# A hybrid decoder layer on one core: a third landing place for x, another step for the value gathers, and the attention's first keys and queries loaded inside the input projection

## The chip, the core and the metric

The kernel runs on one core of a Trainium2 chip. A core has TensorE (PE, matrix products), VectorE (DVE), ScalarE (ACT), GpSimd (POOL) and SyncE (SP, which here only issues transfers); ACT and POOL can issue transfers too. Times are device microseconds (us) of one launch, and the figure compared is the median over runs.

## The reference

One inference step of a one-layer decoder, for a prompt of 2048 new tokens and for 8 samples of 8 new tokens with 8192 cached tokens each. Model width is 1024. Cut to what matters:

```python
z = x @ w_in                                   # one input projection for everything
fq, fk, fv, flogf = ...                        # forgetting attention: 8 heads of 64
mq, mk = silu(conv4(z_qk)); mv, ig, lf, og = ...   # mLSTM: 4 heads of 128
# prompt attention, causal
L = cumsum(flogf)
p = softmax(fq @ fk.T / 8 + L[q] - L[k]);  fox_h = p @ fv
# sample attention over a paged cache (512 pages of 128 tokens) and the 8 new tokens
s_past = q @ k_past.T / 8 + Ln + R;  s_new = ...
p = softmax(concat(s_past, s_new));  o = p @ concat(v_past, v_new)
# mLSTM: chunks of 64 tokens, state C, n, m carried
h = (W * (q @ k.T) @ v + a * q @ C) / den
mix = concat(fox_h, norm(h) * og) @ w_o
x1 = layer_norm(alpha * x + mix)
y  = layer_norm(alpha * x1 + square(relu(x1 @ w1)) @ w2)
```

It returns y for both groups, the new keys, values and log forget values, and the mLSTM and convolution states.

## The kernel before

Precision: every float32 product of the projections is made of three matmuls of split operands (a high and a low part; `split_hi` on ACT, `split_lo` on DVE, both at L154 and L157, the matmuls at L162 to L164). So each weight or x tile is loaded, split on ACT and DVE, and then used by PE.

Stages, in order of time:

- **Input projection**, 0 to about 920 us. The tokens go in four blocks, `BLKS = [[16, 0, 1, 2, 3], [4, 5, 6, 7], [8, 9, 10, 11], [12, 13, 14, 15]]`, where a number is a tile of 128 prompt tokens and 16 stands for the 64 sample tokens. `block_a(bi)` runs, for each block, passes over columns of the weights: mLSTM values (2 passes, with the gates), mLSTM queries and keys (4), output gates (2), attention queries (2) and keys (2), attention values V (2). The passes made token by token go through `natural`, which takes a hook that it calls ahead of each tile; each result is copied from PSUM into a staging tile `st` on ACT and stored. The weights land in `wra` (2 places), loaded by `wload` and split into `whi` and `wlo` (4 places each).
- x lands in the tile `xn`, by `x_load`, issued by SP; `x_turn` splits it into `xh` and `xl`, which the whole block uses. `xn` has 2 landing places, which the gate tiles (`gt`, `rows`) share by their tag.
- Beside the projection's matmuls run two kinds of generators, stepped on by `tick`: `gate_stream`, `m_block` and `m_sample` (mLSTM), and the sample attention (`sample_attention`), which begins in block 0 and runs on in the output projection and the MLP.
- **Prompt attention** `phase_b`, about 920 to 1365 us. It goes over 64 units (8 heads by 8 groups of 256 queries). For each unit: `queries` loads queries (`qn`, two transfers of 64 partitions) and splits them (`qh`, `ql`); `keys` loads 512 keys (`kn`, two transfers) and splits them into `ks`; for the first head it also loads forget values `nl` and values `vn` by pieces of 512 (`forget_values`). `scores` makes `pS` on PE (L945, L946), adds `nl` or the masked diagonal `nd` (made on POOL, L938) and takes row maxima `mx` on DVE; `values` takes the exponential on ACT (S, L973), transposes it on PE (pt, L986) and multiplies with `vn` (po, L995). Scores run one unit ahead of values.
- **Output projection**, about 1365 to 1610 us, and **MLP** to the end.

The sample attention: one `step(n)` after another issues gathers of cached keys (`k_gather`, tile `kT`, L1624) and values (`v_gather`, tile `vt` or `vx`, two gathers each, L1735), both indirect transfers issued by POOL; `qk_step` makes scores (sQ, L1647; sT, L1696), `weights` the transposed probabilities PTs (L1718), and `pv_step` the products with V (sO, L1759). A pair of gathered value tiles has one landing place during the input projection (`vt`) and two afterwards (`vt` and `vx`, once `vx["more"]` is set); `v_room()` says whether one is free. `pv_step` is called at even n from 38 on.

The order on the engines is not the order of the program text: a scheduler lays the instructions out by its own time model, engine by engine, subject to data and to free places, and so carries loads ahead of where they are written. SP runs its queue strictly in order; an entry that waits for its data or for its place holds all that stand behind it. A transfer issued by SP also waits for the eighth transfer before it to have ended, since its completion lanes are used in turn.

At the hand-over from the projection to the prompt attention, block 3's V pass stores 256-wide pieces (`v_prompt`, L574), the last mLSTM chunk makes its output (mn L696, hh on POOL L604, transposed by PE, mm L609, copied by ACT to ot L611, stored to `dmix` L612), and the states C_prompt and n_prompt are stored (L709, L712).

Of the kernel before, what the change touches and what calls it, by code (L numbers as in the profile page):

```python
# [10 lines left out]
F32 = mybir.dt.float32  # L11
# [13 lines left out]
D = 1024  # L25
# [27 lines left out]
def body(ctx, tc, I, O, stages):  # L53
# [152 lines left out]
    for c in W_PASSES:  # L206
        w_at[c] = sum(D * sum(m for _, m in q) for q in w_at)

    es_a = ExitStack()
    pa = es_a.enter_context(tc.tile_pool(name="pa", bufs=1, reuse_waits="tile"))  # L210
# [76 lines left out]
    xns = {}  # L287

    def x_load(*tiles):
        for t in tiles:  # L290
            xns[t] = pa.tile([128, D], F32, name="xn", bufs=2)
            n = 8 * tok_n(t)
            first(SY.dma_start(xns[t][:, :n], I["xs_t"] if t == 16 else I["xp_t"][t]))
# [22 lines left out]
    def gate_stream(bi):  # L316
# [4 lines left out]
        def gates(z, lg, shape, bb):  # L321
            V.tensor_tensor(z, z, bb, op=OP.add)
            gt = pa.tile([128, 1024], F32, name="gt", tag="xn", bufs=2)
            tmp = [gt[:, i * 64:i * 64 + 64].rearrange("p (c g) -> p c g", g=16) for i in range(3)]
# [35 lines left out]
        def rowset(cols, base, n_el, np_, sample):  # L360
            R = [pa.tile([8, 1024], F32, name="rows", tag="xn", bufs=2) for _ in range(2)]
            fr = R[1][:, 0:n_el]
# [73 lines left out]
    def block_a(bi):  # L436
# [18 lines left out]
        def stage(ps, m, n):  # L455
            st = pa.tile([128, 256], F32, name="st", bufs=4)[:m, :n]
            A.copy(st, ps)
            return st

        def turn_next(n):  # L460
            for t in blk[n + 2:n + 3]:
                x_turn(bi, t)
                if bi == 0:
                    x_load(*blk[n + 4:n + 5])

# [105 lines left out]
        for i in range(2):  # L571
            def sink(t, m, ps, i=i):
                d = v_out(t)[:, i * 256:(i + 1) * 256]
                SY.dma_start(d, stage(ps, m, 256))  # L574

            def turn_first(n):
                if n == 0:
                    x_load(*BLKS[bi + 1][0:2])
                if n == len(blk) - 1:
                    x_turn(bi + 1, BLKS[bi + 1][0])  # L580
                    x_load(BLKS[bi + 1][2])
            natural(sink, (1024 + i * 256, 256), hook=None if i == 0 or bi == 3 else turn_first)

# [256 lines left out]
    x_turn(0, 0)  # L840
    x_load(2)
    for bi in range(4):
        g = block_a(bi)
        next(g)
        if bi == 0 and gen:
            acc[0], acc[1] = -12.0, gen
        macc[1].append(m_block(bi))
        mst["open"] = True
        for _ in g:
            pass  # L850
        if bi == 0:
            macc[1].append(m_sample())
        if bi < 3:
            x_turn(bi + 1, BLKS[bi + 1][1])
            x_load(BLKS[bi + 1][3])
    while macc[1]:
# [8 lines left out]
    def phase_b():  # L865
# [47 lines left out]
        def queries(z, g):  # L913

            h = z["h"]
            qn = pb.tile([128, 256], F32, name="qn", bufs=3)
            for d in range(2):
                SY.dma_start(qn[d * 64:d * 64 + 64], dq[h // 2, h % 2 * 64:h % 2 * 64 + 64, g * 256:(g + 1) * 256])
# [108 lines left out]
        Z = {0: dict(h=0)}  # L1027
        kn = keys_load(0, 0)
        queries(Z[0], 0)
# [5 lines left out]
        G.affine_select(dmask, dmask, pattern=[[-1, 128]], compare_op=OP.is_ge, fill=NEG, base=0, channel_multiplier=1)  # L1035
        keys(Z[0], 0, kn)
        sc = {}
        w2_due = [0.0]
        LA = 1
        for n in range(len(units) + LA):  # L1040
# [20 lines left out]
            if n >= LA:  # L1061
                h, g = units[n - LA]
                values(Z[h], g, sc.pop(n - LA))
        es.close()


# [422 lines left out]
def sample_attention(tc, I, O, ps_, pps, cst, ident, dnl, dR, dmix, dqb, vx, kx, pa):  # L1489
# [301 lines left out]
    def step(n):  # L1791
# [3 lines left out]
        g = at(n, 6, 4)  # L1795
# [29 lines left out]
        if g is not None and g < 64:  # L1825
            r_load(g)
        if n >= 35 and (n % 2 == 1 or not vx["live"]):
            while v_room():
                v_gather()
# [73 lines left out]
```

## Time and profile before

| | |
|---|---|
| runs of the kernel | 3286.64, 3292.24, 3301.8 us; median 3292.24 |
| profiled execution | 3288.1 us, span in the profile 3286.4 us |
| PE busy | 3148.6 us (96% of the span), mean granted clock 0.984 |
| DVE, ACT, POOL busy | 2099.1, 1500.7, 912.9 us |
| transfers | 734.37 MB, mean 223 GB/s |
| xn<-xp_t | 16 transfers of 512 KB, SP |
| wra<-w_in | 104 transfers of 512 KB, SP |
| kn<-k_prompt, qn<-dq | 64 of 128 KB, 128 of 64 KB, SP |
| kT gathers, vt gathers (POOL) | 256 and 164, each 1069 ns on POOL |

A line of a group or a timeline reads: start in us (timelines only), time, engine, line, operation, output <- input with its shape, count, and in square brackets the idle time of that engine just before and what ended it. SPq is SP issuing a transfer; its time is that of the issue, with the time for which the queue stood at it, not the transfer's. A row of waits gives the engine and line that waited, what ended the wait, its sum in us, the number of times and the longest.

### The profile page before, as it was taken

The page shows a single profiled execution, that of the slowest core. Times are in us where ns is not written, and L with a number is a line of the kernel's source. Part 1 is how long each engine was busy: PE and PEld are TensorE (multiplying, and loading weights), DVE is VectorE, ACT ScalarE, POOL GpSimd, SP SyncE. Part 2 cuts the span into 40 slices and gives each one's busy share as a digit, 9 for nine tenths or more (in the row PEclk, how much of TensorE's full clock was granted, in tenths as well). Part 3 has the DMA queues.
Part 4 walks back from the last instruction along what each step waited for, and adds up shares of the span by engine and source line. Part 5 has one row for each costly group of instructions (what it writes and reads, how often), then busy time and mean ns, then how long its engine had stood idle before and what let it go on. Part 6 is the DMA issues. An engine that isn't in the chain of part 4 may idle for free.

```text
span 3286.4 us, 58046 instructions
## 1 busy us (share of the span) xinstructions
PE 3148.6 (96%) x21681; PEld 2564.4 (78%) x21681; DVE 2099.1 (64%) x5079; ACT 1500.7 (46%) x2966; POOL 912.9 (28%) x977
## 2 busy tenths in 40 slices
PE   8999998998989999999999999999999999799997
PEld 8998998888856666677677777776777777698895
DVE  6856565355468788644466658656586666856658
ACT  4343343233358888622344345343454444444442
POOL 0121233322324333276433422433333121100000
PEclk9999999999989999999999999999999999999998
DMA  5575766766678675487887878878879666543332
GB/s 186 149 221 177 236 221 216 236 232 198 223 232 226 160 201 136 159 298 253 305 292 273 290 256 298 315 254 327 289 290 343 218 231 211 187 152 119 120 105 100
DMA packets 339698, 734.37 MB, mean 223 GB/s; under 512 B 63640, under 2 KB 177688, under 8 KB 338520
## 3 DMA queue, kind: packets, MB, share of 16 engines
q1 hardware_dynamic: 252856, 416.71, 39.6%
q0 software_dynamic: 83520, 304.12, 26.6%
q10 hardware_dynamic: 3040, 9.83, 0.8%
q8 instruction: 171, 2.80, 0.3%
q14 instruction: 111, 0.91, 0.1%
HBM read 677.71 MB, written 86.38 MB: 233 GB/s over the span
## 4 chain that ended last, share of the span: by engine, by line
PE 45%; DVE 3%; DMA 3%; issue 1%; POOL 1%; ACT 1%; another core or an unknown queue 0%; DVEq 0%; POOLq 0%; ACTq 0%; SPq 0%
PE ph L162 7%; PE ph L163 7%; PE ph L164 7%; PE py L162 6%; PE py L164 5%; PE py L163 5%; PE sO L1759 3%; PE sQ L1647 2%; DMA vt<-cache_v,idxV 1%; DVE wl L157 1%; PE sT L1716 1%; DVE y L1323 1%; DMA kT<-cache_k,idxK 0%; PE pw L163 0%; PE pw L164 0%
## 5 line engine op out<-in xcount | busy, mean ns | idle before, releaser
L157 DVE TENSOR_TENSOR wl<-wr,wh 128x1024 fp32r<-128x1024 f32 x364 | 445.6, 1226 | 376.3 <-ACT wh L154 341.0
L154 ACT ACTIVATE wh<-wr 128x1024 fp32r<-128x1024 f32 x364 | 382.6, 1054 | 321.8 <-PE ph L163 131.1
L162 PE MATMUL ph<-x1h,wh 128*128 128x512 f32 (+1 forms) x1280 | 455.8, 356 | 0.8 <-DVE x1l L157 0.5
L163 PE MATMUL ph<-x1l,wh 128*128 128x512 f32 (+1 forms) x1280 | 453.9, 355 | 0.0
L1624 POOL DMA_INDIRECT kT<-cache_k,idxK x256 | 273.7, 1069 | 640.0 <-PE sQ L1647 578.0
L164 PE MATMUL ph<-x1h,wl 128*128 128x512 f32 (+1 forms) x1280 | 451.3, 354 | 0.0
L162 PE MATMUL py<-wh,hh 128*128 128x512 f32 x896 | 356.8, 400 | 5.9 <-DVE y L1323 2.5
L163 PE MATMUL py<-wl,hh 128*128 128x512 f32 x896 | 351.6, 392 | 0.3 <-issue 0.3
L164 PE MATMUL py<-wh,hl 128*128 128x512 f32 x896 | 349.6, 393 | 1.3 <-DVE hl L157 1.0
L1323 DVE TENSOR_TENSOR y<-y,py 128x512 f32<-128x512 f32 x416 | 280.3, 682 | 69.0 <-PE py L164 55.7
L162 PE MATMUL pm<-xh,whi 128*128 128x256 f32 (+1 forms) x1024 | 301.7, 295 | 1.3 <-issue 0.8
L163 PE MATMUL pm<-xl,whi 128*128 128x256 f32 (+1 forms) x1024 | 297.6, 291 | 2.3 <-issue 2.2
L164 PE MATMUL pm<-xh,wlo 128*128 128x256 f32 (+1 forms) x1024 | 296.8, 290 | 2.8 <-issue 2.8
L162 PEld LDWEIGHTS ph<-x1h,wh 128*128 128x128 f32 x1280 | 241.3, 189 | 40.9 <-issue 7.8
L1735 POOL DMA_INDIRECT vt<-cache_v,idxV x164 | 175.3, 1069 | 340.5 <-PE sO L1759 272.6
L163 PEld LDWEIGHTS ph<-x1l,wh 128*128 128x128 f32 x1280 | 241.5, 189 | 34.2 <-issue 3.7
L164 PEld LDWEIGHTS ph<-x1h,wl 128*128 128x128 f32 x1280 | 241.0, 189 | 34.1 <-issue 3.7
L162 PE MATMUL pm<-whi,xh 128*128 128x256 f32 (+2 forms) x816 | 238.7, 293 | 9.2 <-ACT whi L154 8.3
L163 PE MATMUL pm<-wlo,xh 128*128 128x256 f32 (+2 forms) x816 | 233.9, 287 | 1.6 <-issue 1.0
L164 PE MATMUL pm<-whi,xl 128*128 128x256 f32 (+2 forms) x816 | 233.5, 286 | 0.9 <-issue 0.8
L973 ACT ACTIVATE S<-S,mx 128x512 f32<-128x512 f32 (+2 forms) x320 | 207.8, 653 | 18.2 <-DVE mx L959 15.8
L162 PEld LDWEIGHTS py<-wh,hh 128*128 128x128 f32 x896 | 168.3, 188 | 55.5 <-issue 14.0
(371 smaller groups left out, 6810.5 us busy)
## 6 DMA issues: line engine op xcount, KB each, us to landing
wr<-w SPq DMA_DIRECT2D x224, 512.0 KB
wr<-dw SPq DMA_DIRECT2D x128, 512.0 KB
wra<-w_in SPq DMA_DIRECT2D x104, 512.0 KB
dw<-w POOLq DMA_DIRECT2D x48, 512.0 KB
Rb<-dR SPq DMA_DIRECT2D x128, 128.0 KB
xn<-xp_t SPq DMA_DIRECT2D x16, 512.0 KB
kn<-k_prompt SPq DMA_DIRECT2D x64, 128.0 KB
qn<-dq SPq DMA_DIRECT2D x128, 64.0 KB
```

The lines of the kernel that those rows point to most:

```text
L154: last["ACT"] = A.activation(dst, src, AF.Copy, scale=scale)
L157: r = (eng or V).tensor_tensor(dst, src, hi.bitcast(F32), op=OP.subtract)
L162: T.matmul(ps, wh, xh, start=first, stop=False, skip_group_check=shared)
L163: T.matmul(ps, wh, xl, start=False, stop=False, skip_group_check=shared)
L164: last["PE"] = T.matmul(ps, wl, xh, start=False, stop=stop, skip_group_check=shared)
L973: last["ACT"] = A.activation(sp[:, :w], sp[:, :w], AF.Exp, bias=mx[:, 7:8], accum_out=lp[:, k:k + 1])
L1323: V.tensor_tensor(y, y, ps, op=op)
L1624: G.indirect_dma_start(out=piece(n), out_offset=None, in_=ck, in_offset=IO(ap=idxK[:, b, j // 2, j % 2:j % 2 + 1], axis=0))
L1647: r = T.matmul(pq[h4 * 32:h4 * 32 + 32, hg].rearrange("p (k c) -> p k c", k=2), z["qb"][:, hd], kv, start=(db == 0), stop=(db == 1), skip_ ...
L1716: T.transpose(p[:, f], z["U"][u][:, hg, f].rearrange("p k t -> p (k t)"), ident)
L1735: G.indirect_dma_start(out=vt.rearrange("p f c -> p (f c)"), out_offset=None, in_=cv, in_offset=IO(ap=idxV[:, b, (kt % 4) * 4 + kt // 4, f ...
L1759: after_ = T.matmul(po[r:r + 32], z["PT"][:, hg, 2 * f + g, pg].rearrange("p h q -> p (h q)"), vts[f][:, g, hg * 256:(hg + 1) * 256], star ...
```

## The change

Four edits.

1. `xn`, `gt` and `rows` get 3 places instead of 2 (4 KB of each partition). x loads move: of the next block, two tiles are loaded during the first V pass and one during the second, and the fourth at its end, when the first of them is split; before, two were loaded at the second V pass's first tile, one at its end and one at the block's turn. In block 0 tile 3 is loaded before the block begins, not in its first pass.
2. In `step`, values are gathered at even n instead of odd n when a place is free and another is in use. In the text of `step` the value gathers stand ahead of the key gathers as before.
3. `begin_b` loads the first keys (128x512) and the first queries (128x256) of the prompt attention into tiles of their own (pool `pf`, 3 KB of each partition), from a hook in block 3's last V pass; the attention no longer loads them.
4. The stores of block 3's last V pass are issued by ACT instead of SP.

```diff
+    es_f = ExitStack()
+    pf = es_f.enter_context(tc.tile_pool(name="pf", bufs=1, reuse_waits="tile"))
+    bf = {}
+
+    def begin_b():
+
+        bf["kn"] = pf.tile([128, 512], F32, name="kn0")
+        bf["qn"] = pf.tile([128, 256], F32, name="qn0")
+        for d in range(2):
+            SY.dma_start(bf["kn"][d * 64:d * 64 + 64], O["k_prompt"][0:64, 0:512])
+        for d in range(2):
+            SY.dma_start(bf["qn"][d * 64:d * 64 + 64], dq[0, 0:64, 0:256])
...
-            xns[t] = pa.tile([128, D], F32, name="xn", bufs=2)
+            xns[t] = pa.tile([128, D], F32, name="xn", bufs=3)
...
-            gt = pa.tile([128, 1024], F32, name="gt", tag="xn", bufs=2)
+            gt = pa.tile([128, 1024], F32, name="gt", tag="xn", bufs=3)
...
-            R = [pa.tile([8, 1024], F32, name="rows", tag="xn", bufs=2) for _ in range(2)]
+            R = [pa.tile([8, 1024], F32, name="rows", tag="xn", bufs=3) for _ in range(2)]
...
         def turn_next(n):
             for t in blk[n + 2:n + 3]:
                 x_turn(bi, t)
-                if bi == 0:
-                    x_load(*blk[n + 4:n + 5])
...
                 d = v_out(t)[:, i * 256:(i + 1) * 256]
-                SY.dma_start(d, stage(ps, m, 256))
-
-            def turn_first(n):
-                if n == 0:
-                    x_load(*BLKS[bi + 1][0:2])
-                if n == len(blk) - 1:
+                (A if bi == 3 and i == 1 else SY).dma_start(d, stage(ps, m, 256))
+
+            def turn_first(n, i=i):
+                if n % 2 == len(blk) % 2:
+                    if i == 0 or n < 2:
+                        x_load(BLKS[bi + 1][(i * 2 + n // 2) if n < 4 else 1])
+                if i == 1 and n == len(blk) - 1:
                     x_turn(bi + 1, BLKS[bi + 1][0])
-                    x_load(BLKS[bi + 1][2])
-            natural(sink, (1024 + i * 256, 256), hook=None if i == 0 or bi == 3 else turn_first)
+                    x_load(BLKS[bi + 1][3])
+
+            def b_first(n, i=i):
+                if i == 1 and n == 0:
+                    begin_b()
+            natural(sink, (1024 + i * 256, 256), hook=b_first if bi == 3 else turn_first)
...
     x_load(2)
+    x_load(3)
...
         if bi < 3:
             x_turn(bi + 1, BLKS[bi + 1][1])
-            x_load(BLKS[bi + 1][3])
...
-            qn = pb.tile([128, 256], F32, name="qn", bufs=3)
-            for d in range(2):
+            qn = bf["qn"] if h == g == 0 else pb.tile([128, 256], F32, name="qn", bufs=3)
+            for d in range(2 if h or g else 0):
...
-        kn = keys_load(0, 0)
...
-        keys(Z[0], 0, kn)
+        keys(Z[0], 0, bf["kn"])
...
-        if n >= 35 and (n % 2 == 1 or not vx["live"]):
+        if n >= 35 and (n % 2 == 0 or not vx["live"]):
             while v_room():
                 v_gather()
```

More of the change, by code (lines that the diff above doesn't have):

```diff
@@ L1064, in phase_b @@
         es.close()
+        es_f.close()
     dmv = dmix.rearrange("j p t -> p j t")
```

## The prediction

> **What bounds the kernel now.** I read the page first, then the waits of TensorE (PE) by stretch, then the timeline where PE stood still.
>
> ```profile
> span 3286.4 us, 58046 instructions
> PE 3148.6 (96%) x21681; PEld 2564.4 (78%) x21681; DVE 2099.1 (64%) x5079; ACT 1500.7 (46%) x2966; POOL 912.9 (28%) x977
> PE 45%; DVE 3%; DMA 3%; issue 1%; POOL 1%; ACT 1%; another core or an unknown queue 0%; DVEq 0%; POOLq 0%; ACTq 0%; SPq 0%
> ```
>
> PE is busy 3148.6 of 3286.4 us and leads the chain that ended last. No matrix product goes, so all that can be won lies in the 137.8 us in which PE stands and in the matmuls at a lowered clock behind. First the input projection (0 to 920 us), with one row of ACT's below PE's; the columns are the sum, the number and the longest of the waits.
>
> ```profile
> PE sO L1759 <- DMA vt<-cache_v,idxV: 11.5, 3, 8.2
> PE sT L1696 <- ACT PTs L1718: 6.8, 1, 6.8
> PE pm L164 <- issue: 3.6, 5, 1.1
> PE pm L163 <- issue: 3.2, 7, 0.8
> ACT xh L154 <- DMA xn<-xp_t: 6.0, 6, 1.6
> ```
>
> Then the 50 us in which it hands over to the prompt attention (900 to 950 us).
>
> ```profile
> PE pS L945 <- ACT qh L154: 4.0, 1, 4.0
> PE pt L986 <- ACT S L973: 3.4, 2, 3.2
> PE mm L609 <- POOL hh L604: 2.8, 1, 2.8
> ```
>
> Three places matter: one stand of 8.2 us for gathered values, one of 6.8 us behind ACT, and about 10 us at the hand-over. Waiting for x itself is cheap: ACT's row shows 6.0 us in six waits, and ACT has slack. Half a per cent, 16.5 us, is about the least that a measurement of this kernel tells from no change.
>
> **Part 1: keys and queries of the first unit loaded early, last V stores from ACT's queue.** The timelines of SyncE (SP, which issues loads), ACT, POOL and PE over the hand-over:
>
> ```profile
> 911.85 7.85 SPq L574 DMA_DIRECT2D v_prompt<-st  x3
> 922.56 0.33 SPq L712 DMA_DIRECT2D n_prompt<-nn  x1
> 924.37 0.38 SPq L612 DMA_DIRECT2D dmix<-ot  x1
> 924.79 0.51 SPq L918 DMA_DIRECT2D qn<-dq  x1
> 925.39 0.54 SPq L894 DMA_DIRECT2D nl<-dnl  x1
> 926.46 1.15 SPq L900 DMA_DIRECT2D kn<-k_prompt  x2
> 928.76 2.43 SPq L918 DMA_DIRECT2D qn<-dq  x4
> ```
>
> ```profile
> 923.76 0.58 ACT L611 COPY ot<-mm 128x512 f32<-128x512 f32 x1 [4.41 <-PE mm L609]
> 927.21 0.42 ACT L154 ACTIVATE qh<-qn 128x256 fp32r<-128x256 f32 x1 [2.34 <-DMA qn<-dq]
> 931.05 0.63 ACT L154 ACTIVATE ks<-kn 128x512 fp32r<-128x512 f32 x1 [3.43 <-DMA kn<-k_prompt]
> 933.32 0.42 ACT L154 ACTIVATE qh<-qn 128x256 fp32r<-128x256 f32 x1 [0.42 <-DMA qn<-dq]
> 929.18 0.86 POOL L938 TENSOR_TENSOR nd<-nl,dmask 128x128 f32<-128x128 f32 x2 [6.43 <-DMA nl<-dnl]
> ```
>
> ```profile
> 922.56 1.12 PE L609 MATMUL mm<-ident,hh 128*128 128x128 f32 x4 [2.77 <-POOL hh L604]
> 927.68 0.79 PE L945 MATMUL pS<-ks,qh 128*128 128x256 f32 x2 [4.00 <-ACT qh L154]
> 932.12 1.18 PE L986 MATMUL pt<-ident,S 128*128 128x128 f32 x3 [3.19 <-ACT S L973]
> 934.88 1.12 PE L945 MATMUL pS<-ks,qh 128*128 128x384 f32 x2
> ```
>
> SP stands in the V stores until 911.85 + 7.85 = 919.7, each of which waits for its copy on ACT; behind them come the first keys, then two state stores that wait for their data (n_prompt is the second), then the first queries, of which the second half stands behind the dmix store until 924.79. So PE's first scores start at 927.68, and the forget values (nl) that the mask sum on POOL needs land at 929.18.
>
> After the change four small loads stand in the first token block, hundreds of microseconds ahead. They are two issues of keys (1.15 us by their row) and two of queries (2.43 / 2 = 1.2), 2.4 us on a queue that is ahead of PE there: nothing on the path. At the hand-over ACT splits queries and keys right after the last V copy, with no load to wait for; in the order of the built program PE then does the four transposes of mm before the first scores. Those end at 922.56 + 1.12 = 923.68. So the first scores move from 927.68 to 923.7, a gain of 4.0. In the new order nl stands on SP ahead of the state stores, right behind a dmix store at some 909 us, so the mask is there as soon as it is wanted.
>
> What is late next: the second piece of keys. It is issued behind n_prompt, which ends at 922.56 + 0.33, instead of at 926.46; its landing took 931.05 - 926.46 = 4.6 us, so ACT's split goes from 931.05 to 927.5, 3.6 earlier, and the transposes behind the second exponential go with it. The second unit's queries were issued at 928.76 and split at 933.32, 4.6 us later. In the new order they stand behind the dmix store, one nl and one vn, so at about 924.8 + 2 x 0.55 = 925.9: 2.9 earlier. The three thus move by 4.0, 3.6 and 2.9. I take 4, by the row of PE's wait (4.00), and keep 1 to 6 as ends: 1 if the later queries set the pace and land no sooner, 6 if PE's second wait (3.19) shrinks besides. The V stores moved to ACT are four issues of about 0.4 us there between copies that ACT waits for anyway (it stood 4.41 us before ot): nothing.
>
> The Trainium skill ("DMA: Bandwidth & Descriptors", "Issuing engines are not separate DMA queues") says that starting transfers from several engines saves only the sequencer's time to start them. By that, moving four stores off SP is worth their issue time alone, 4 x 0.4 = 1.6 us; the rows above speak against it, since the wait of 7.85 us over three stores is SP standing in order behind ACT, not starting transfers.
>
> **The clock behind it.** Windows of 5 us (PE busy, PEld, DVE, ACT, POOL, then the granted clock of PE):
>
> ```profile
> 920.00:925.00 5.00, 1.12 (x4) 0.72 (x4) 2.63 (x11) 1.11 (x2) 1.51 (x2) 0.70 0.47 145
> 935.00:940.00 5.00, 4.75 (x13) 2.91 (x13) 3.07 (x14) 2.18 (x6) 1.51 (x3) 0.59 1.04 353
> 520.00:525.00 5.00, 3.35 (x16) 3.27 (x17) 2.92 (x3) 2.93 (x7) 0.00 (x0) 0.50 0.44 161
> ```
>
> PE's clock stands at half in about 922 to 938 us. Of the matmuls there only the dense ones from 934.88 on bound anything; in 935 to 940 PE was busy 4.75 us at a mean of 0.59, so at most 4.75 x 0.41 = 1.95 us were lost. With stands some 4 us shorter the clock should rise as much earlier: I take 1.5, with 0 as one end and as the other what all four windows from 920 to 940 could give back, which the two shown bound by (1.12 + 4.75) / 2 = 2.9.
>
> The Trainium skill ("TensorE: Matmul & The Clock Gate", "What's actually happening") states that the clock falls to half after one idle window of about 3.4 us. By that the only stand left before the first scores (2.77 us before mm) would not trip it and the whole 2.9 would come back; but in the first window the mean is already 0.70 with that stand and no longer one before 923.7, so the trace does not agree and I stay at 1.5.
>
> **Part 2: third landing place for x.** Between two token blocks the kernel now has three x tiles in flight ahead of the turn instead of two, and loads the fourth there; before, two were issued at each turn. In the built order SP's queue differs little: in the third block the x loads and weight loads (wra) still alternate as in the rows below, behind the same two broadcast loads. Only the place for x is free earlier. In all of the projection the idles that ended by "issue" (the two rows of pm above) are 3.6 + 3.2 us in twelve pieces, and x cost ACT at most 1.6 at a time. Three of the twelve follow the third turn within 15 us, none the other two: by number a quarter, 1.7 us. I take 2 as the gain, 0 and 6.8 as its ends. The extra load's issue of some 0.45 us (row of xn below) is hidden in SP's waits; not hidden, the three of them would cost 1.4.
>
> What does not go, on my reading, is the 6.8 us stand. Timeline of SP, then of ACT:
>
> ```profile
> 506.91 0.45 SPq L293 DMA_DIRECT2D xn<-xp_t  x1
> 507.93 4.79 SPq L293 DMA_DIRECT2D xn<-xp_t  x1
> 512.77 12.78 SPq L262 DMA_DIRECT2D wra<-w_in  x3
> 520.38 1.06 ACT L154 ACTIVATE whi<-wra 128x1024 fp32r<-128x1024 f32 x1 [10.93 <-DMA wra<-w_in]
> ```
>
> ACT stood 10.93 us for a weight tile that was issued between the two x loads, and the transposes of PE behind it 6.8. The x loads and broadcasts stay in front of it in the new order, so I leave this at 0.
>
> **Part 3: the gathers of values.** The edit swaps the parity of the step in which POOL issues gathers of V. While only one landing place is free for them (all of the projection) the other half of the condition is true whenever they can go, so nothing moves there; in the built order POOL's gathers there stand as before. The largest wait stays:
>
> ```profile
> 745.67 2.44 POOL L1624 DMA_INDIRECT kT<-cache_k,idxK  x1 [17.01 <-PE sQ L1647]
> 752.88 0.94 POOL L1735 DMA_INDIRECT vt<-cache_v,idxV  x1 [0.30 <-issue]
> 769.72 1.94 PE L1759 MATMUL sO<-vt,PTs 128*32 128x256 f32 x16 [8.16 <-DMA vt<-cache_v,idxV]
> ```
>
> In the output projection and the MLP, where two places are free, the built order still has four gathers of keys and then the values; the steps of the sample attention stand one step (some 24 matmuls) earlier against the weights' matmuls. All waits of PE for values there are 17.8 us of the kernel less the 11.5 shown, 6.3; the change can take them or add as many. I take 0, with -6 and +6 as ends.
>
> ```profile
> PE sO L1759 <- DMA vt<-cache_v,idxV: 17.8, 7, 8.2
> ```
>
> **Sum.** -4 (hand-over) - 1.5 (clock) - 2 (turns) + 0 (values) = -7.5 us. The profiled execution took 3288.1 us (span 3286.4), so it would take 3280.6; it lies 4.1 under the median of the runs, 3292.24, from which the sum gives 3284.7. I say 3284. The ends add up to -21.7 and +5, so the case's own range is about 3270 to 3297.
>
> **Rivals.**
> - *The third place clears SP's queue (faster).* If the x load that took 4.79 us in SP's queue goes before the broadcasts, the weights behind it land in time. That takes 6.8 us and the half clock behind: PE was busy 3.35 us at 0.50 in 520 to 525, as much again lost as 3.35 x 0.5 = 1.7. So -8.5 beside the -7.5 makes 3276; if moved traffic also brings the values of 769.72 in time (8.16, and by the same proportion 1.7 for the clock), -9.9 more, 3266. For it: SP's stand is at an x load. Against it: the new order keeps that load behind the broadcasts. 0.33, since the lanes' timing is not in the order.
> - *Nothing at the hand-over.* The first scores go earlier, but the second keys and queries arrive with the same traffic and PE waits there as long. Then -2 from the turns remains: 3290. Against it: ACT's rows above are released by loads that stood behind others in SP's queue. 0.10. The Trainium skill's rule on issuing engines, quoted above, comes out beside this case: with its 1.6 us for the hand-over, 3288.6.
> - *The extra x load takes the weights' place in the queue (slower).* An x tile asked for before its place is free holds SP, and the weight loads behind it, as the row of 4.79 us shows. If it happens at the head of the first block (one more load is issued there) and at the three turns, each gives a stand like the one at 521 us: 6.8 + 1.7 = 8.5. One cancels the gain (3293), two make 3302, three 3310, four 3319. It decides where ACT's wait for weights passes 10.93 - 6.8 = 4.1 us, since that much was hidden there. For it: three x tiles in flight put one more in front of the weights at each turn. Against: the order alternates x and weights as before. 0.21.
>
> That the edit of the gathers does not do what its words say (keys still go first) is already the forecast's zero.
>
> **How the numbers follow.** Forecast 0.36 (of it 0.06 below 3275.8, the bound of faster), clearing 0.33 (0.03 above that bound; over half of it has more than the one stand), nothing gained 0.10, weights delayed 0.21 (0.01 inside the bound: its weight is on three places and more). Faster 0.06 + 0.30 = 0.36; slower than 3308.7 0.20; the same 0.44. The range takes in the forecast, the lower of the clearing's times with 4 us of uncertain values below it, 3262, and the rival's three places, 3310.
>
> **What would show it.** Right: in the changed profile no idle ended by qh before the first pS, first scores within 5 us of the last mn and some 4 us nearer to it than before; nl issued right behind a dmix store before C_prompt; the wait for vt at about 770 and the wait of 6.8 us on PTs in the third block still there. Wrong: if those two are gone (clearing), if the waits of ACT for wra have grown beside xn issues of several us on SP (delay), or if the second ks and qh on ACT still stand for loads as long as before.

## The result, and the profile after

| | before | changed |
|---|---|---|
| median of the runs | 3290.21 us (4 runs, 3286.64 to 3301.80) | 3310.71 us (4 runs, 3308.74 to 3316.66) |
| profiled execution | 3288.1 us, span 3286.4 | 3316.66 us, span 3315.0 |

The ratio on record is 1.0071, with a 95% interval of 1.0048 to 1.0094 (the two medians alone give 1.0062): the changed kernel is slower by some 20 us. The forecast was 3284, faster by 8; the range ended at 3310, 0.7 below the result. The profiled execution of the changed kernel is the slowest of its four, so its trace holds some 6 us that the median does not. From the page of the changed kernel:

```profile
span 3315.0 us, 58020 instructions
...
PE 3157.1 (95%) x21681; PEld 2571.6 (78%) x21681; DVE 2097.4 (63%) x5079; ACT 1502.4 (45%) x2966; POOL 906.1 (27%) x977
```

The matmuls are the same 21681. PE is busy 8.5 us longer (the same work at a lower clock, 0.981 after 0.984) and idle 157.9 instead of 137.8 us. To see where, I paired equal VectorE instructions of two traces and took the median of (start in the kernel - start in before) in slices of 20 us, for this kernel and for those of the experiments below. A row is a place in the time of before:

```
at us   after   e1     e2     e3     e6     e9     e7     e7c    e15
 140     1.3    0.0   -1.1    0.0   -1.0   -1.3    0.0    0.7    1.0
 200     6.8    0.3   -1.2    7.7   -0.3   -0.7   -1.0   -0.1    0.9
 900     1.2  -10.9   -2.0    3.3    1.6   -5.4   -7.0   -3.3  -25.6
1000    -1.6   -8.4   -0.1    0.1   -1.8   -4.6   -5.6   -2.0  -25.2
1360     8.4   -7.0    0.1    2.6    4.2   -3.1   -5.3   -2.3  -24.0
1540     8.8   -7.7   -0.4    5.5    3.1   -4.4   -5.6   -0.1  -25.2
2060    26.6    9.6   -2.3   -1.6    5.3   14.6  -10.3    0.7  -33.8
2400    25.7    5.7    2.1    7.9    4.9   10.2   -9.8    3.5  -40.2
2600    27.2    9.1   10.2   14.1    4.8   13.5    8.7    5.2  -41.1
2940    28.2    8.8   10.5   15.0    5.5   16.2   11.6    6.3  -41.5
```

The column "after" has three steps up: 5.5 us between 140 and 200 us, 10 us inside the prompt attention (1000 to 1360), and 17.8 us between 1540 and 2060, from the end of the output projection to the second block of the MLP. At the hand-over it falls by 2.8. One caution on such columns: e1 differs from before in nothing that runs before 1380 us, and still stands at -10.9 by 900. The long waits of the input projection come and go by some 10 us from execution to execution, so only steps that several kernels share, or that the medians confirm, count here.

The first step needs that care too, since the column "after" is back at 1.2 by 900 us. Three kernels took the step and have not the order of the last experiments (after, e3 and e4, by the same pairing): at 900 us they stand at -2.3 to 3.3, on average 0.7. The eleven others without that order stand at -13.1 to 1.6, on average -5.4. So before's own execution was slow in between, and some 6 us of the step may be left; among the four kernels with the order the one that took the step (e17) is less than 1 us behind the mean of the rest.

**The first step.** SP's timeline, before and then after:

```profile
138.91 0.80 SPq L567 DMA_DIRECT2D dq<-st  x2
140.49 0.32 SPq L569 DMA_DIRECT2D dqb<-qr  x1
...
141.41 0.39 SPq L634 DMA_DIRECT2D Wm<-dM  x1
```

```profile
140.19 0.80 SPq L578 DMA_DIRECT2D dq<-st  x2
145.47 1.14 SPq L220 DMA_DIRECT2D qn<-dq  x2
146.70 0.54 SPq L580 DMA_DIRECT2D dqb<-qr  x1
...
147.83 0.40 SPq L650 DMA_DIRECT2D Wm<-dM  x1
```

The early query load (qn, L220) reads what the two dq stores just ahead of it write. SP ended issuing them at 140.99 and could issue the load at 145.47, 4.5 us later; the rest of the queue stood behind. What SP waited for, 138 to 150 us, after:

```profile
SPq L220 <- DMA dq<-st: 4.4, 1, 4.4
```

Wm, an mLSTM load that has nothing to do with it, went out 6.4 us later than before, 1.3 of which the kernel was behind already. Its chain ends in a wait of PE that before did not have (waits of PE, 130 to 210 us, after):

```profile
PE mm L625 <- POOL hh L620: 4.9, 1, 4.9
```

The Trainium skill ("DMA: Bandwidth & Descriptors", "Two DMAs through the same engine are not ordered") tells the author to let the issuing engine wait for the first transfer's semaphore before a transfer that depends on it. The trace agrees, and shows the price: that wait is 4.5 us long, and it is the whole queue that waits.

**The hand-over.** PE, then ACT, after:

```profile
919.95 1.05 PE L712 MATMUL mn<-va,kw 128*128 128x129 f32 x8
923.78 0.66 PE L625 MATMUL mm<-ident,hh 128*128 128x128 f32 x4 [2.77 <-POOL hh L620]
924.96 0.58 PE L961 MATMUL pS<-ks,qh 128*128 128x256 f32 x1 [0.52 <-DVE ks L157]
...
935.15 1.54 PE L961 MATMUL pS<-ks,qh 128*128 128x384 f32 x3 [2.15 <-ACT qh L154]
```

```profile
929.48 0.63 ACT L154 ACTIVATE ks<-kn 128x512 fp32r<-128x512 f32 x1 [2.16 <-DMA kn<-k_prompt]
...
934.68 0.42 ACT L154 ACTIVATE qh<-qn 128x256 fp32r<-128x256 f32 x1 [1.26 <-DMA qn<-dq]
```

Counted from the last mn (918.73 before, 919.95 after) the first scores come at 5.0 instead of 8.95 us: 3.9 earlier. The second keys are split at 9.5 instead of 12.3, 2.8 earlier; but the second unit's queries are split at 14.7 instead of 14.6, no earlier at all, and that unit's scores gain 1.0.

**The third step.** Waits of PE, 1545 to 2110 us: the changed kernel, and the same kernel without the edit of the value gathers.

```profile
PE px L1157 <- DVE x1l L157: 5.8, 1, 5.8
PE sO L1775 <- DMA vt<-cache_v,idxV: 4.4, 1, 4.4
PE sQ L1663 <- DMA kT<-cache_k,idxK: 4.3, 2, 3.4
PE px L1157 <- DMA xr<-dx: 3.4, 2, 2.5
PE py L162 <- DVE y L1339: 3.0, 3, 1.5
```

```profile
PE px L1157 <- DVE x1l L157: 3.9, 1, 3.9
PE sO L1775 <- DMA vx<-cache_v,idxV: 2.5, 1, 2.5
PE sQ L1663 <- DMA kT<-cache_k,idxK: 2.1, 2, 1.8
PE sO L1775 <- DMA vt<-cache_v,idxV: 0.7, 2, 0.5
```

With the edit the waits for x1l and for keys are longer, those for values come to 4.4 us in place of 2.5 and 0.7, and two are new: the one for y, and the one for the rows of x for the next MLP block (xr<-dx), whose landing place is the second landing place of the values. In all PE stands 27.3 of these 565 us, and 9.8 without the edit; the difference of 17.5 is the step.

### The profile page after: what moved, and what is told of

Read it like the earlier page. It is cut to its first block, busy times and chain, and to the rows that moved or that the text cites. A ratio compares the mean times of both kernels' runs of the same rounds, so it can differ in the third digit from the quotient of the medians.

```text
span 3315.0 us, 58020 instructions
## 1 busy us (share of the span) xinstructions
PE 3157.1 (95%) x21681; PEld 2571.6 (78%) x21681; DVE 2097.4 (63%) x5079; ACT 1502.4 (45%) x2966; POOL 906.1 (27%) x977
## 4 chain that ended last, share of the span: by engine, by line
PE 47%; DMA 2%; DVE 2%; issue 1%; another core or an unknown queue 0%; POOL 0%; ACT 0%; DVEq 0%; SPq 0%; POOLq 0%
PE ph L162 8%; PE ph L164 8%; PE ph L163 8%; PE py L162 6%; PE py L164 6%; PE py L163 6%; PE sO L1775 3%; PE sQ L1663 2%; DMA vt<-cache_v,idxV 1%; DMA xr<-dx 1%; PE sT L1732 1%; DVE y L1339 1%; DVE wl L157 0%; DMA kT<-cache_k,idxK 0%
## 5 line engine op out<-in xcount | busy, mean ns | idle before, releaser
L157 DVE TENSOR_TENSOR wlo<-wra,whi 128x1024 fp32r<-128x1024 f32 (+1 forms) x112 | 140.8, 1260 | 111.6 <-ACT whi L154 109.8
```

The source lines that it names most:

```text
L157: r = (eng or V).tensor_tensor(dst, src, hi.bitcast(F32), op=OP.subtract)
```

## The experiments

Each is compared with before on the same chip (5 rounds).

| | edit | ratio to before | 95% interval |
|---|---|---|---|
| e1 | values at even n alone | 1.0046 | 1.0027 to 1.0066 |
| e2 | third place for x alone | 1.0011 | 0.9996 to 1.0025 |
| e3 | early keys, V stores on ACT | 1.0030 | 1.0014 to 1.0045 |
| e4 | all but the values | 1.0041 | 1.0022 to 1.0060 |
| e5 | changed kernel, early loads held late | 1.0051 | 1.0037 to 1.0066 |
| e6 | e3, early loads held late | 1.0019 | 1.0008 to 1.0030 |
| e10 | e6, V stores on SP | 1.0011 | 0.9996 to 1.0026 |
| e13 | before, with the attention's last product (output by reciprocal sums) on VectorE instead of POOL | 1.0132 | 1.0113 to 1.0151 |
| e12 | e6 with the same | 1.0125 | 1.0104 to 1.0147 |
| e9 | one forced step, odd n | 1.0071 | 1.0055 to 1.0087 |
| e7 | even n, no forced step | 1.0071 | 1.0057 to 1.0085 |
| e7c | e7, closed early at all turns | 1.0024 | 1.0009 to 1.0039 |
| e14 | odd n, closed early at all turns | 1.0009 | 0.9998 to 1.0020 |
| e15 | values really ahead of keys | 0.9869 | 0.9851 to 0.9888 |
| e16 | e7c with that order | 0.9863 | 0.9845 to 0.9881 |
| e17 | changed kernel with that order | 0.9926 | 0.9910 to 0.9942 |
| e18 | e5, odd n, with that order | 0.9896 | 0.9874 to 0.9917 |

### Each part by itself: e1, e2, e3, e4

The hunks are those of the diff; e1 is one line:

```diff
-        if n >= 35 and (n % 2 == 1 or not vx["live"]):
+        if n >= 35 and (n % 2 == 0 or not vx["live"]):
```

Expected of e1:

> The kernel before with the one edit of the value gathers (even n instead of odd n), nothing else. Theory V: the loss lies in the stages where values have two landing places (output projection and MLP). Against matched VectorE instructions the changed kernel falls behind by about 4 us between 1550 and 1620 us and by some 15 more up to 2850 us, so this kernel alone should be slower by 12 to 20 us (3302 to 3310). Theory B (the loss comes from the prompt attention, which the early keys re-ordered): no change, within 4 us of 3290. Theory X (the third place for x moved the sample attention's steps for good): no change here either.

Expected of e2:

> The kernel before with the third landing place for x and its loads moved, nothing else. Theory V and theory B: within 4 us of 3290 (in the changed kernel the input projection loses 7 us near 170 us, has them back by 640 us, and ends level with before). Theory X: slower by 10 us or more (3300 and up), since the steps of the sample attention that follow all shift.

Expected of e3:

> The kernel before with the first keys and queries of the attention loaded early and the last V stores issued by ACT, nothing else. Theory V: faster by 2 to 4 us (3287), the gain at the hand-over that the changed kernel shows (offset from +1.2 at 900 to -1.8 at 1000 us). Theory B: slower by 5 to 8 us (3297), because in the changed kernel the prompt attention gives back 10 us between 1150 and 1365 us. Theory X: as V.

Expected of e4:

> The changed kernel without the edit of the value gathers (odd n as before). Theory V: 3287 to 3298, that is the changed kernel less 12 to 20 us. Theory B: about 3307 less nothing, within 5 us of the changed kernel. Theory X: as B.

The edit of the values costs 0.46% alone (15 us) and 0.3% on top of the others; theory V holds for its part. The early keys cost 0.30% (10 us), so theory B, or something like it, holds besides. The third place for x cannot be told from nothing. The three add to 0.87%, near the 0.71 measured; each of the three is known to within 0.2% only.

### Where the early loads stand: e5, e6, e10

```diff
+    def behind(r):
+        tc.add_manual_dep(r.ins, bf["last"].name, <order only>)
...
-            SY.dma_start(bf["qn"][d * 64:d * 64 + 64], dq[0, 0:64, 0:256])
+            behind(SY.dma_start(bf["qn"][d * 64:d * 64 + 64], dq[0, 0:64, 0:256]))
```

and the same for kn; `bf["last"]` is the last store of keys of the fourth block. e10 puts the V stores back on SP.

Expected of e5:

> The changed kernel with one thing altered: the four early loads of keys and queries are ordered behind the last store of keys of the fourth block, instead of in the first block. Theory Q (SP stood at the query load at 140 to 145 us until the stores that it reads had landed, and the mLSTM's loads behind it were late by 6 us, for which PE stood 4.9 us): the offset of 5 to 7 us that the changed kernel takes on between 145 and 200 us is gone, and the kernel is 5 to 8 us faster than the changed one (0.2 per cent: ratio to before about 1.005). Rival (the loss is in the re-ordered prompt attention): ratio stays at 1.007.

Expected of e6:

> The early keys alone (with the V stores on ACT), held behind the last store of keys of the fourth block. Theory Q: 7 to 8 us faster than the same edit without the hold (ratio 1.003), and the gain at the hand-over remains, so 2 to 5 us faster than before (ratio 0.9985 to 0.9995). Rival (prompt attention re-ordered): ratio stays at 1.002 to 1.003.

Expected of e10:

> The early keys alone, held behind the last store of keys of the fourth block, with the last V stores issued by SP as before. If the hand-over's gain comes from the V stores that no longer hold SP: the first exponentials wait for nl again and the gain at the hand-over (4.6 us with the stores on ACT) falls to 1 to 3, so the kernel is 2 to 3 us slower than with them (ratio 1.0025). If it comes from the early keys and queries alone: as with them, ratio 1.002.

SP's timeline of e5 at the same place, and the waits of PE from 130 to 210 us:

```profile
139.29 0.36 SPq L583 DMA_DIRECT2D dq<-st  x1
139.75 0.38 SPq L657 DMA_DIRECT2D Wm<-dM  x1
```

```profile
PE mm L700 <- DVE Wm L690: 0.7, 1, 0.7
PE mm L632 <- POOL hh L627: 0.5, 1, 0.5
```

The queue runs through, the wait of 4.9 us is down to 0.5, and the step at 140 to 200 us is gone from the column of e6. e5 is 0.20% under the changed kernel, as theory Q said, and e6 is 0.11% under e3, half of what it said; in both pairs the intervals overlap, so it is the traces that show the step, and its worth in the median is not settled. But e6 is still slower than before, where a gain was expected. Its column says why: from 900 to 1000 it falls by 3.4 (the hand-over), from 1000 to 1360 it gives back 6.0. The stores on ACT bring nothing that can be told in the medians (e10 1.0011, e6 1.0019); in the one trace of each the hand-over gains 1.8 us in e10 and 3.4 in e6.

### Why the attention gives the gain back: e12, e13

```diff
-                G.tensor_tensor(ot[:, s], ot[:, s], rl, op=OP.mult)
+                V.tensor_tensor(ot[:, s], ot[:, s], rl, op=OP.mult)
```

In the changed kernel, VectorE, POOL and PE around one stand of PE in the attention:

```profile
1275.19 2.96 DVE L157 TENSOR_TENSOR ql<-qn,qh 128x256 fp32r<-128x256 f32 x1
...
1278.77 0.14 DVE L975 TENSOR_REDUCE mx<-mx 128x1 f32<-128x4 f32 x1
```

```profile
1276.00 1.86 POOL L1037 TENSOR_TENSOR ot<-ot,rl 64x512 f32<-64x512 f32 x1
```

```profile
1278.90 1.58 PE L1002 MATMUL pt<-ident,S 128*128 128x128 f32 x8 [2.54 <-DVE mx L975]
```

A split of queries that takes 0.42 us stretched to 2.96 beside POOL's product (ot); the maximum behind it (mx) came late, ACT's exponential and PE's transposes with it. The longest wait of PE from 1150 to 1365 us in sum, in the changed kernel and then in before:

```profile
PE pt L1002 <- DVE mx L975: 4.2, 2, 2.5
```

```profile
PE pt L986 <- DVE PT L991: 1.1, 3, 0.5
```

Both waits for mx stand right behind a long split (2.00 and 2.96 us): 4.2 of the 10 us that the attention gives back. e6 has one such wait, 2.2 of its 6.0. What makes up the rest stays open. That the early loads bring it is plain all the same: between 1000 and 1360 us the eight kernels that have them and leave the product on POOL fall back by 2.5 to 11.8 us, and eight without them by -0.3 to 1.5.

Expected of e13:

> The kernel before with that product moved from POOL to VectorE: the other half of the pair. In the kernel before the splits beside the product took up to 1.85 us and PE hardly stood for them, so within 5 us of before by theory C and by its rival; VectorE has some 20 us more to do in the attention, where it is busy 82 per cent.

Expected of e12:

> The early keys held late, and the product of the attention's output with the reciprocal sums moved from POOL to VectorE. Theory C (in the re-ordered attention VectorE's split of queries, 0.42 us alone, falls beside POOL's product and takes 2.6 us, which holds up a maximum and PE): the 4 to 6 us that the kernel lost between 1050 and 1365 us are gone, and against the kernel before with the same product on VectorE it is 2 to 5 us faster. Rival (the new order itself costs): it stays 4 to 6 us slower than that kernel.

e13 missed: the move costs some 43 us by itself, and by that neither is a better kernel. The 32 products keep VectorE busy 21.7 us, but more goes to its standing in front of them until the reciprocal sums (rl) have landed, with the maxima that PE waits for behind. VectorE's longest wait in sum from 920 to 1420 us in e13:

```profile
DVE ot L1021 <- DMA rl<-drl: 48.6, 15, 7.8
```

So the pair is a weak test of theory C. e12 (3323.93) is 3.8 us under e13 (3327.76), with intervals that overlap. Paired with each other, e12 goes from +4.6 at 900 to -0.8 at 1000 and -3.4 at 1350, so in the attention the gain is not given back; but by 2000 us the two traces are level (0.3), and in both VectorE stands for rl (48.6 and 45.7 us), which it does not in before or e6. That is some support, not proof.

### What the edit of the values does: e9, e7, e7c, e14

At the end of the output projection the kernel takes the second landing place back (`take_back`) and, while a pair of values is still in it, runs steps of the sample attention out of turn. By the kernels' own bookkeeping before runs none there or at the MLP's turns. With even n one pair is there, one step is run, and nearly all later steps stand one step earlier against the matmuls of the MLP. The traces agree: counted in matmuls of the weights, most steps of e1 and of the changed kernel behind that place begin 18 to 36 earlier than in before, and those of e4 at the same place as in before. e9 does that to the kernel before; e7 keeps even n and closes the place earlier there and in the first MLP block, so that none is run at these two; e7c closes it earlier at every turn; e14 is e7c with odd n.

```diff
+        attend()                                   # e9, behind take_back() in the output projection
...
-            if t == 13:                            # e7, e7c, e14
+            if t == 12:
                 vx["more"] = None
...
-                if p == 6:                         # e7 for ci == 0 only; e7c, e14 always
+                if p == 5:
                     vx["more"] = None
```

Expected of e9:

> The kernel before, value gathers at odd n, with one step of the sample attention run out of turn at the end of the output projection, as happens with even n. Theory S: slower by 8 to 16 us (ratio 1.0025 to 1.005), although no gather was moved to another step. Theory P: no change (ratio within 0.0012 of 1).

Expected of e7:

> The kernel before with the value gathers at even n, and with the second landing place closed one token tile earlier at the end of the output projection and one piece earlier in the first MLP block, so that no pair of values is still in the second place when it is taken back. Theory S (at the end of the output projection a pair is still in the second place with even n, so one step of the sample attention is run out of turn there, and all later steps stand one step earlier against the MLP's work): the loss is gone, within 4 us of before (ratio 0.999 to 1.001). Theory P (gathering at even n is itself bad): ratio stays at about 1.0045.

Expected of e7c:

> As the kernel with the values at even n and no forced step, but the second landing place for values is closed one piece earlier before each turn of the MLP's blocks, not only the first. That kernel kept level with before up to 2400 us and lost 18 us between 2420 and 2520 us, at the second turn. Theory T (at a turn, a pair of values gathered late into the second place, which the residual rows of x share, holds up those rows): the 18 us are gone, ratio to before 0.999 to 1.002. Rival P (even n is bad by itself): the ratio stays at 1.007.

Expected of e14:

> The kernel before (values at odd n) with the second landing place closed one tile and one piece earlier before each turn: the control of the kernel with even n closed early (ratio 1.0024). If even n is harmless once no pair stands in the way of a turn, this control has the same ratio, 1.001 to 1.003 (the closing costs the 0.2 per cent). If even n has a cost of its own, the control is at 0.999 to 1.001 and the remaining 0.2 per cent belong to even n.

Waits of PE in e9, 1545 to 2110 us:

```profile
PE sQ L1648 <- DVE rl L1707: 7.0, 3, 5.6
PE sO L1760 <- DMA vt<-cache_v,idxV: 6.7, 1, 6.7
PE px L1141 <- DMA xr<-dx: 4.3, 1, 4.3
PE sQ L1648 <- DMA kT<-cache_k,idxK: 4.0, 1, 4.0
```

With no gather moved to another step, one step forced there, with what it brings at later turns, costs 0.71% and brings waits like those of the changed kernel (for values, for keys and the new one, xr<-dx) and the same climb between 1540 and 2060 (19.0 us; after 17.8, e1 17.3). In e7 that climb is gone (-4.7), as theory S said, but the kernel is no faster: it loses 18.5 us between 2400 and 2600, at the second turn of the MLP (e2 and e3, which the edit does not touch, lose 6 to 8 against before there, so some 10 are its own). Its trace says why: from 2406 to 2521 us its steps begin 20 to 84 matmuls of the weights earlier than those of before, and those of e7c do not, so at that turn, which e7 does not close early, a step was run out of turn after all. Waits of PE there (2400 to 2540 us), e7 and then e7c:

```profile
PE sO L1759 <- DMA vt<-cache_v,idxV: 8.4, 2, 7.2
PE px L1141 <- DVE ln_rs L173: 3.5, 1, 3.5
PE ph L162 <- DVE x1l L157: 3.1, 1, 3.1
```

```profile
PE sO L1759 <- DMA vt<-cache_v,idxV: 2.4, 1, 2.4
PE sO L1759 <- DMA xr<-cache_v,idxV: 2.0, 1, 2.0
```

Closed early at that turn too, the kernel has 15 us of it back (e7c 1.0024). So with even n a late pair of values collides with a turn, now at one place, now at another. What is left of the 0.24% against e14's 0.09% is within the intervals: whether even n costs anything of its own stays open. With the order tried next, even n (e16) and odd n (e15) come out level.

### Values really ahead of keys: e15, e16, e17, e18

```diff
-        G.indirect_dma_start(out=piece(n), ... in_=ck, ...)
+        r = G.indirect_dma_start(out=piece(n), ... in_=ck, ...)
+        if "last" in vx:
+            tc.add_manual_dep(r.ins, vx["last"].name, <order only>)
```

`vx["last"]` is the last gather of values issued in the program text. e16 is e7c with it, e17 the changed kernel, e18 e5 with odd n.

Expected of e15:

> The kernel before with what the words of the change say really made: each gather of keys is ordered behind the gathers of values that the program text has ahead of it, so that POOL's queue goes keys, keys, values, values instead of four keys and then four values. Theory G (the values' place in POOL's queue is what PE waits for): the waits of sO for values after 1400 us (6 us in before) go, ratio 0.997 to 0.999. Theory H (the gathers of keys then stand behind values that wait for the place of a product not yet done): waits of sQ for kT grow by more than that, ratio 1.001 to 1.005.

Expected of e16:

> Even n, second place closed early before every turn, and the gathers of keys ordered behind the values ahead of them in the program text. Theory G: 0.2 per cent or more faster than the same without that order (ratio 1.0024 before), so 0.998 to 1.0005. Theory H: slower than it, 1.003 and more.

Expected of e17:

> The changed kernel, all four edits, with each gather of keys ordered behind the gathers of values ahead of it in the program text. If the order's gain adds to the change as it stands (ratio 1.007 and the order's 0.987), 0.993 to 0.996. If the order also takes away what the shifted steps cost (PE's waits for values and for rows after 1550 us), 0.988 to 0.992.

Expected of e18:

> The third place for x, the early keys held late with the V stores on ACT, values at odd n, and the order of values ahead of keys. By the parts alone (1.001, 1.002 and 0.987): 0.989 to 0.991. If the parts that cost in the attention or at the turns cost nothing once the sample attention is in time: 0.985 to 0.988, level with the order alone or better.

POOL's timeline of e15, at the place of the 8.2 us wait of before (there four gathers of keys stood ahead of the values):

```profile
729.52 1.17 POOL L1738 DMA_INDIRECT vt<-cache_v,idxV  x1 [18.94 <-PE sO L1762]
730.99 1.20 POOL L1738 DMA_INDIRECT vt<-cache_v,idxV  x1 [0.30 <-issue]
732.50 1.26 POOL L1624 DMA_INDIRECT kT<-cache_k,idxK  x1 [0.30 <-issue]
```

The page of e15, and the waits of PE over its whole span:

```profile
span 3244.9 us, 58028 instructions
...
PE 3132.3 (97%) x21681; PEld 2557.2 (79%) x21681; DVE 2095.2 (65%) x5079; ACT 1501.7 (46%) x2966; POOL 919.4 (28%) x977
```

```profile
PE sO L1762 <- DMA vt<-cache_v,idxV: 8.6, 4, 5.3
...
PE sQ L1650 <- DMA kT<-cache_k,idxK: 5.2, 4, 2.6
```

e15 takes 3245.70 us, 1.3% under before, e16 3243.03: both beat both kernels, by far more than theory G allowed (0.1 to 0.3%). PE idles 112.6 instead of 137.8 us, and is busy 16.3 less, at a clock of 0.988. The waits for values fall from 17.8 to 8.6 us, those for keys rise from 3.8 to 5.2. These rows carry only a part of the 41.5 us between the spans. The column places most of it: 25.6 us are won by 900 us, nearly all of them between 560 and 900, and some 10 more between 1920 and 2160. The same work of the projection, in before and then in e15 (PE is the first engine, its granted clock the third number from the end):

```profile
560.00:900.00 340.00, 314.77 (x2797) 288.59 (x2799) 159.28 (x457) 114.22 (x252) 100.81 (x113) 0.95 0.69 227
```

```profile
558.80:874.40 315.60, 304.87 (x2794) 282.60 (x2796) 158.67 (x455) 113.87 (x252) 110.81 (x115) 0.98 0.73 246
```

There PE stands 10.7 instead of 25.2 us, and is busy 9.9 us less at a higher clock. All four kernels with the order stand at -25.4 to -28.5 by 900 us, the others no lower than -13.1. So the larger part of the gain lies in the input projection, where the change's edit of the values moves nothing. e17 shows that the order adds to the change as it stands (0.9926; 1.0071 times 0.9869 is 0.9939). e18 (0.9896) is no better than the order alone: the change's other parts add nothing.

## Why the prediction was wrong, point by point

- **Early loads, "two issues of keys and two of queries on a queue that is ahead of PE there: nothing on the path".** This step failed. Their issue is cheap; what I left out is that the query load reads the store just ahead of it and so holds the queue until that has landed: 4.5 us in the trace, 5.5 us of PE by 200 us, of which 1 to 6 are left at the end of the projection. The working saw that the scheduler had carried the loads into the first block and took "hundreds of microseconds ahead" for "free".
- **Hand-over, -4 and -1.5.** The mechanism and its first term were right: first scores 3.9 us earlier for 4.0, second keys 2.8 for 3.6. The second unit's queries, 2.9 earlier by the sum, were issued 2.4 us earlier against the last mn, but took 7.1 us from there to the split instead of the 4.6 that the sum took over from before, and so came no earlier; the column above shows -2.8 for the hand-over in all. The clock's term had the wrong sign. The clock rose later, not sooner: the granted clock was 0.50 in 935 to 940 us (0.59 before), and in 940 to 945 us it was 0.51 in the changed kernel and 1.00 before, as the last row of each fence shows. PE was busy all 5 us of that window, so up to 5.00 x 0.49 = 2.5 us went there, by my estimate:

```profile
935.00:940.00 5.00, 3.57 (x9) 2.47 (x10) 3.18 (x13) 1.78 (x5) 0.92 (x2) 0.50 0.87 266
940.00:945.00 5.00, 5.00 (x18) 4.30 (x19) 4.24 (x22) 4.11 (x13) 1.86 (x5) 0.51 1.10 357
```

```profile
940.00:945.00 5.00, 4.46 (x27) 3.13 (x27) 4.80 (x27) 4.66 (x15) 2.37 (x5) 1.00 1.09 361
```

- **What the attention does with a new start** had no term. Its order changes with the edit, and it gives back 2.5 (e3), 6.0 (e6) and 10.0 us (changed kernel), in part where VectorE's splits fall beside POOL's product (4.2 us in the changed kernel, 2.2 in e6); the rest stays open.
- **Values, "0, with -6 and +6 as ends".** The largest miss: 10 to 15 us by the medians (e1, and after against e4). That keys still go first was right (e15 shows what it costs). That the later steps stand one step earlier was seen and written down, and priced by the waits for values that before had. This step failed: the price is at the turns, in a landing place shared with x, and in the clock behind those waits (0.98 in the changed kernel and 0.97 in e1 from 1545 to 2110 us, 0.99 before).
- **Third place for x, -2.** Not there: e2 is 1.0011, 0.9996 to 1.0025. The two stands that I expected to stay did stay (7.3 us on PTs in the third block, 8.0 us on vt near 770).
- **The slower rival** had the right sign and the right resource, SP's queue held by an entry that waits, but put it on an x load; it was the query load, and it explains a quarter of the loss at most. That the result lies beside this rival's time for three places, 3310, is chance.
- **The rule of the Trainium skill ("DMA: Bandwidth & Descriptors", "Issuing engines are not separate DMA queues") that issuing from several engines saves only the time to start transfers** I weighed lightly, on the wait of 7.85 us. The runs do not speak against it: with the V stores on SP the kernel is no slower (e10 against e6).

## What to carry to other kernels

A load moved early is not free because it is early: ask which store it reads, and what stands behind it in its queue until that store has landed. When an edit moves a background activity by one step, price every place where the two meet again (turns, shared landing places), not the waits that exist now. And where program text asks for an order that the scheduler does not keep, the order may be worth having: here one ordering dependence from values to keys gave 1.3%, while the change, which moved the gathers to another step without that order, was part of what made the kernel 0.7% slower. A product moved to another engine takes its wait along: on VectorE the wait for rl (48.6 us) was more than the products themselves (21.7 us).

## What the runs showed of the hardware that I had not expected

VectorE's split of two SBUF operands (ql, 128x256) and POOL's elementwise work hold each other up: beside the split of 2.96 us POOL's product took 1.86 us, where most of its 32 take 1.27. Over the attention of eight of the kernels, with early keys or without, the split took at most 0.53 us where no POOL product or mask sum ran (24 to 27 of some 63 in each), and up to 3.01 us beside POOL's product. POOL's issuing of loads (dw) is not enough for it: beside such an issue alone the split took at most 0.53 us. The Trainium skill ("SBUF — State Buffer", "SBUF: two separate sides") says that the port pair that the two share is an exclusive lock, and that a VectorE instruction with two SBUF inputs and a GpSimd one that reads SBUF block each other for a whole instruction. The traces agree in part. The stretch of 2.5 us is there, but not every time: beside the product the median was 0.5 to 1.3 us. And by the rows above the split began 0.8 us ahead of the product that it seems to have waited for, while POOL was still issuing two loads; the spans on POOL are rough, so who came first is not shown.
